# Loading two small tables from the same DMA queue as the data, ahead of it

## Chip, cores, metric

One core of a Trainium2 chip; the other cores are idle. The metric is the device time of one execution in microseconds (us), the median of several executions. A profile of one execution is read beside it; its span, counted from the first instruction, is some 2 us shorter than the time.

## The reference

The input `x` has shape (16, 512, 16, 64) in float32, 33.6 MB. `cos` and `sin` have shape (512, 32), 64 KB each. Only the first 32 values of each head are rotated; the other 32 are copied.

```python
x1, x2 = x[..., :32], x[..., 32:]
first  = x1[..., :16] * cos[..., :16] - x1[..., 16:] * sin[..., :16]
second = x1[..., :16] * sin[..., :16] + x1[..., 16:] * cos[..., :16]
return np.concatenate([first, second, x2], axis=-1)
```

All of `x` has to be read and all of the output written: 67.1 MB.

## The kernel before

`x` is cut into 8 tiles of 4 MB, 128 partitions by 32 KB. A tile is loaded through SP's DMA queue, rotated in place on VectorE in two halves (two products, a difference and a sum each), and stored through ACT's queue. Five buffers rotate, so the first five loads need not wait for a store. The tables are loaded once, through ACT's queue, and spread by VectorE into `table`.

```python
stage = const_pool.tile([PB, 2, K, HF], fp32)            # PB = 64 partitions
nc.scalar.dma_start(out=stage[:, 0]..., in_=cosf)        # ACT's queue
nc.scalar.dma_start(out=stage[:, 1]..., in_=sinf)
table = const_pool.tile([P, 2, K, 2, Q], fp32)
# ... four tensor_copy of stage into table ...
for t in range(T):                                       # 8 tiles
    x_t = x_pool.tile([P, K, H, D], fp32)                # bufs=5
    nc.sync.dma_start(out=x_t..., in_=xf[t])             # SP's queue
    for k0 in range(0, K, KC):
        # ... a = x1*c; b = x1*s; x1 = a-b | a+b, on VectorE ...
    nc.scalar.dma_start(out=of[t], in_=x_t...)           # ACT's queue
```

Of the kernel before, what the change touches and what calls it, by code (L numbers as in the profile page):

```python
# [1 line left out]

# [4 lines left out]


@with_exitstack
def kernel(  # L10
    ctx: ExitStack,
    tc: tile.TileContext,
    x: bass.AP,
    cos: bass.AP,
    sin: bass.AP,
    out: bass.AP,
):
    nc = tc.nc
    fp32 = mybir.dt.float32
    P = 128  # L20
    B, S, H, D = x.shape
    Q = D // 4
    HF = D // 2


    K = 8
    T = B * S // (P * K)
    PB = S // K
    REP = P // PB

    xf = x.rearrange("b s h d -> (b s h d)").rearrange("(t p f) -> t p f", t=T, p=P)
    of = out.rearrange("b s h d -> (b s h d)").rearrange("(t p f) -> t p f", t=T, p=P)
    cosf = cos.rearrange("(p k) j -> p (k j)", k=K)
    sinf = sin.rearrange("(p k) j -> p (k j)", k=K)

    const_pool = ctx.enter_context(tc.tile_pool(name="const", bufs=1))
    x_pool = ctx.enter_context(tc.tile_pool(name="xp", bufs=5))
    ab_pool = ctx.enter_context(tc.tile_pool(name="abp", bufs=1))

    stage = const_pool.tile([PB, 2, K, HF], fp32)  # L40
    nc.scalar.dma_start(out=stage[:, 0].rearrange("p k j -> p (k j)"), in_=cosf)  # L41
    nc.scalar.dma_start(out=stage[:, 1].rearrange("p k j -> p (k j)"), in_=sinf)


    table = const_pool.tile([P, 2, K, 2, Q], fp32)
    for r in range(REP):
        for t in range(2):
            nc.vector.tensor_copy(  # L48
                out=table[r * PB : (r + 1) * PB, t],
                in_=stage[:, t, :, 0:Q].unsqueeze(2).to_broadcast((PB, K, 2, Q)),  # L50
            )
    C = table[:, 0].rearrange("p k c j -> p k (c j)")
    Sn = table[:, 1].rearrange("p k c j -> p k (c j)")

    KC = 4
    for t in range(T):
        x_t = x_pool.tile([P, K, H, D], fp32)
        nc.sync.dma_start(out=x_t.rearrange("p k h d -> p (k h d)"), in_=xf[t])  # L58
        for k0 in range(0, K, KC):
            x1 = x_t[:, k0 : k0 + KC, :, 0:HF]  # L60
            c = C[:, k0 : k0 + KC].unsqueeze(2).to_broadcast((P, KC, H, HF))
            s = Sn[:, k0 : k0 + KC].unsqueeze(2).to_broadcast((P, KC, H, HF))
            a_t = ab_pool.tile([P, KC, H, HF], fp32)
            b_t = ab_pool.tile([P, KC, H, HF], fp32)
            nc.vector.tensor_mul(out=a_t[:], in0=x1, in1=c)  # L65
            nc.vector.tensor_mul(out=b_t[:], in0=x1, in1=s)  # L66
            nc.vector.tensor_sub(  # L67
                out=x1[:, :, :, 0:Q], in0=a_t[:, :, :, 0:Q], in1=b_t[:, :, :, Q:HF]
            )
            nc.vector.tensor_add(  # L70
                out=x1[:, :, :, Q:HF], in0=a_t[:, :, :, Q:HF], in1=b_t[:, :, :, 0:Q]
            )
        nc.scalar.dma_start(out=of[t], in_=x_t.rearrange("p k h d -> p (k h d)"))


# [1 line left out]
_INS = ['x', 'cos', 'sin']  # L77
_OUTS = [((16, 512, 16, 64), 'float32')]


# [23 lines left out]
```

## Time and profile before

| | before |
|---|---|
| time, median of 3 | 162.38 us (162.28 to 162.39) |
| VectorE busy | 110.8 us, 69% of the span |
| data moved, mean rate | 67.25 MB, 419 GB/s |
| first and last DMA packet (packet records) | 1.73 us, 159.2 us |
| one 32 KB packet on one of 16 DMA engines, median | 1.213 us, so 432 GB/s for all 16 |

From the page of the kernel before: the span; VectorE's busy time; then three rows with one entry for each of 40 slices of the span (VectorE's and the DMA engines' busy share in tenths, and the GB/s moved); then the chain of work that ended last, by engine and by line.

```profile
span 160.4 us, 155 instructions
...
DVE 110.8 (69%) x68; POOL 0.2 (0%) x4
...
DVE  0001599999999999999998799609995099940000
...
DMA  7999999999999999999999999999999999999993
GB/s 253 408 400 408 392 417 490 400 408 498 400 400 474 433 392 457 457 392 449 466 392 417 490 400 408 498 400 400 476 425 400 466 441 400 449 457 400 417 482 147
...
DMA 53%; DVE 30%; issue 4%; DVEq 1%; ACTq 0%; SPq 0%
DMA x_t<-in_x_dram 21%; DMA out_dram<-x_t 21%; DVE b_t L66 11%; DMA stage<-in_sin_dram 10%; DVE a_t L65 10%; DVE x_t L70 5%; DVE x_t L67 4%; DVEq L99 1%; ACTq L41 0%; DVE table L48 0%; SPq L58 0%; DVEq L65 0%
```

The DMA row is the one to read. It is at 9 in every slice but the first and the last: the 16 engines have no spare time. VectorE's row is empty for the first three slices and has gaps later. An idle VectorE costs something only if it leaves the DMA engines without work. The chain also names the load of sin (10%), which is what draws the eye to the tables. Single slices of the GB/s row swing by some 10 to 15% because the engines' 32 KB packets run nearly in step.

VectorE's waits in the kernel before: who waited for what, us in total, times, longest.

```profile
DVE a_t L65 <- DMA x_t<-in_x_dram: 13.2, 3, 5.9
DVE table L48 <- DMA stage<-in_cos_dram: 12.2, 1, 12.2
DVE table L48 <- DMA stage<-in_sin_dram: 4.9, 1, 4.9
```

The start of the timeline before: start in us, duration in us, engine, line, operation; in brackets the idle time before it and what ended it. A `q` marks an engine's sequencer issuing a DMA.

```profile
0.73 0.54 ACTq L41 DMA_DIRECT2D stage<-in_cos_dram  x1
0.73 11.78 SPq L58 DMA_DIRECT2D x_t<-in_x_dram  x5
1.30 0.61 ACTq L42 DMA_DIRECT2D stage<-in_sin_dram  x1
12.19 0.59 DVE L48 COPY table<-stage 64x256 f32<-64x256 f32 x2 [12.19 <-DMA stage<-in_cos_dram]
17.67 0.59 DVE L48 COPY table<-stage 64x256 f32<-64x256 f32 x2 [4.90 <-DMA stage<-in_sin_dram]
18.29 2.29 DVE L65 TENSOR_TENSOR a_t<-x_t,table 128x2048 f32<-128x2048 f32 x1
...
32.14 0.35 ACTq L73 DMA_DIRECT2D out_dram<-x_t  x1
```

SP and ACT start to issue at the same moment, 0.73 us. The tables land at 12.2 and 17.6 us, and the first product starts at 18.29 us. Tile 0 of `x` had landed at 13.62 us. The first store is issued at 32.14 us.

DMA issues before: KB each, and the median time from issue to landing in us.

```profile
x_t<-in_x_dram SPq DMA_DIRECT2D x8, 4096.0 KB, 33.9
out_dram<-x_t ACTq DMA_DIRECT2D x8, 4096.0 KB, 31.3
stage<-in_cos_dram ACTq DMA_DIRECT2D x1, 64.0 KB, 11.4
stage<-in_sin_dram ACTq DMA_DIRECT2D x1, 64.0 KB, 16.3
```

A 64 KB table needs 11 to 16 us. The packet records say why: its first packet runs at 5.95 us, behind three 32 KB packets of `x` on each engine (48 have started by then on the 16 engines), and after that each engine mostly runs one 1 KB table packet (46 ns) and then one of `x`.

### The profile page before, as it was taken

To read this page: it belongs to the slowest core of one execution; us is meant where nothing else is said; L and a number is where in the kernel's file an instruction comes from. 1 tells how busy PE (TensorE), PEld (TensorE's weight loads), DVE (VectorE), ACT (ScalarE), POOL (GpSimd) and SP (SyncE) were. 2 spreads that over 40 slices of the span, in tenths; PEclk is the share of its full clock that TensorE was granted. 3 is DMA by queue.
4 is the path that set the end of the run, shared out by engine and by line. 5 is a ranking of instruction groups with operands and counts; after the bars stand their busy time and mean duration, and the time that the engine had idled before them with its cause. 6 is when DMAs were issued, how large, how long until landed. Compare 5 with 4: busy or idle time off the path is not lost.

```text
span 160.4 us, 155 instructions
## 1 busy us (share of the span) xinstructions
DVE 110.8 (69%) x68; POOL 0.2 (0%) x4
## 2 busy tenths in 40 slices
DVE  0001599999999999999998799609995099940000
POOL 0000000000000000000000000000000000000000
DMA  7999999999999999999999999999999999999993
GB/s 253 408 400 408 392 417 490 400 408 498 400 400 474 433 392 457 457 392 449 466 392 417 490 400 408 498 400 400 476 425 400 466 441 400 449 457 400 417 482 147
DMA packets 2465, 67.25 MB, mean 419 GB/s; under 512 B 288, under 2 KB 416, under 8 KB 416
## 3 DMA queue, kind: packets, MB, share of 16 engines
q1 hardware_dynamic: 1152, 33.55, 49.3%
q10 hardware_dynamic: 1312, 33.69, 48.7%
q14 instruction: 1, 0.01, 0.0%
HBM read 33.69 MB, written 33.55 MB: 419 GB/s over the span
## 4 chain that ended last, share of the span: by engine, by line
DMA 53%; DVE 30%; issue 4%; DVEq 1%; ACTq 0%; SPq 0%
DMA x_t<-in_x_dram 21%; DMA out_dram<-x_t 21%; DVE b_t L66 11%; DMA stage<-in_sin_dram 10%; DVE a_t L65 10%; DVE x_t L70 5%; DVE x_t L67 4%; DVEq L99 1%; ACTq L41 0%; DVE table L48 0%; SPq L58 0%; DVEq L65 0%
## 5 line engine op out<-in xcount | busy, mean ns | idle before, releaser
L65 DVE TENSOR_TENSOR a_t<-x_t,table 128x2048 f32<-128x2048 f32 x16 | 36.7, 2292 | 13.6 <-DMA x_t<-in_x_dram 13.2
L66 DVE TENSOR_TENSOR b_t<-x_t,table 128x2048 f32<-128x2048 f32 x16 | 36.5, 2284 | 0.0
L67 DVE TENSOR_TENSOR x_t<-a_t,b_t 128x1024 f32<-128x1024 f32 x16 | 19.6, 1226 | 0.6
L70 DVE TENSOR_TENSOR x_t<-a_t,b_t 128x1024 f32<-128x1024 f32 x16 | 19.5, 1218 | 0.0
L48 DVE COPY table<-stage 64x256 f32<-64x256 f32 x4 | 1.1, 287 | 17.1 <-DMA stage<-in_cos_dram 12.2
L88 POOL MEMSET const-bfloat16-1.0<- 128x1 bf16 x1 | 0.1, 102 | 0.0
L88 POOL MEMSET const-uint8-127<- 128x1 uint8 x1 | 0.1, 102 | 0.0
L88 POOL MEMSET const-float32-0.0<- 128x1 f32 x1 | 0.1, 99 | 0.2 <-issue 0.2
L88 POOL MEMSET const-float32-1.0<- 128x1 f32 x1 | 0.1, 99 | 0.0
## 6 DMA issues: line engine op xcount, KB each, us to landing
x_t<-in_x_dram SPq DMA_DIRECT2D x8, 4096.0 KB, 33.9
out_dram<-x_t ACTq DMA_DIRECT2D x8, 4096.0 KB, 31.3
stage<-in_cos_dram ACTq DMA_DIRECT2D x1, 64.0 KB, 11.4
stage<-in_sin_dram ACTq DMA_DIRECT2D x1, 64.0 KB, 16.3
```

Of the source, the lines that this page charges most:

```text
L48: nc.vector.tensor_copy(out=table[r * PB : (r + 1) * PB, t], in_=stage[:, t, :, 0:Q].unsqueeze(2).to_broadcast((PB, K, 2, Q)),)
L65: nc.vector.tensor_mul(out=a_t[:], in0=x1, in1=c)
L66: nc.vector.tensor_mul(out=b_t[:], in0=x1, in1=s)
L67: nc.vector.tensor_sub(out=x1[:, :, :, 0:Q], in0=a_t[:, :, :, 0:Q], in1=b_t[:, :, :, Q:HF])
L70: nc.vector.tensor_add(out=x1[:, :, :, Q:HF], in0=a_t[:, :, :, Q:HF], in1=b_t[:, :, :, 0:Q])
L88: nc = _bacc.Bacc("TRN2", target_bir_lowering=False, num_devices=1)
L99: with _tile.TileContext(nc) as tc:
```

## The change

The intent is to have the tables before the first tile of `x`, so that VectorE, and with it the first store, starts earlier. Both table loads move from ACT's queue to SP's, ahead of the loads of `x`.

```diff
     stage = const_pool.tile([PB, 2, K, HF], fp32)
-    nc.scalar.dma_start(out=stage[:, 0].rearrange("p k j -> p (k j)"), in_=cosf)
-    nc.scalar.dma_start(out=stage[:, 1].rearrange("p k j -> p (k j)"), in_=sinf)
+    nc.sync.dma_start(out=stage[:, 0].rearrange("p k j -> p (k j)"), in_=cosf)
+    nc.sync.dma_start(out=stage[:, 1].rearrange("p k j -> p (k j)"), in_=sinf)
```

## The prediction

> **What bounds the kernel now.** The 16 DMA engines. The page's DMA row shows 9 tenths in all slices but the first and last, and 419 GB/s over the span of 160.4 us. In the trace's packet records the first packet starts at 1.73 us and the last ends at 159.2, with hardly a gap; summed packet time is 157.0 us per engine. A 32 KB packet takes 1.213 us on one engine, so 16 engines move 432 GB/s. That is near the 435 GB/s fabric ceiling in the Trainium skill, page "DMA: Bandwidth & Descriptors", section "Where 436 GB/s comes from"; this trace agrees. 2048 such packets over 16 engines are 155.3 us. VectorE is busy 110.8 us (69%): not the limit.
>
> The chain of waits does begin with the sin table (16.3 us, until 17.65), and the list of waits has VectorE waiting 12.2 us for cos and 4.9 us for sin, although x tile 0 landed at 13.62 us. That wait is the change's aim.
>
> **What the change does.** It adds and removes no work. The table issues move from ACT's queue to SP's, ahead of the x loads.
> - Before, SP's first x issue and ACT's cos issue both started at 0.73 us, and the first x packet ran 1.0 us later. Now x follows two table issues. An x issue took 0.33 us alone and 0.37 to 0.67 in company, so I estimate that x starts 0.7 to 0.9 us later.
> - The table packets (128 of 1 KB, 46 ns each: 0.37 us per engine) fill part of that gap; before, they ran between x packets. The net loss of about 0.4 us is on the critical path, since DMA is saturated from there to the end.
>
> Gain: tables land at about 4 us, so the first product starts when x tile 0 lands, about 14.3 us instead of 18.3, and the first store is issued at about 28.3 us instead of 32.1.
>
> **What that is worth.** Nearly nothing. Earlier stores take turns with loads on full engines: the same page, section "Issuing engines are not separate DMA queues", says that transfers of all queues interleave on the same engines. The trace agrees: 432 GB/s in loads alone, about 216 + 216 mixed, 433 in stores alone. The loads therefore end later by about the 3.8 us by which stores start earlier: the last load lands near 132 us instead of 128.2, the last store is issued near 146 instead of 142.1. Its predecessor lands near 150 us (149.95 before), so the store queue still doesn't run dry: its slack shrinks from 7.8 to about 4 us.
>
> **Predicted time:** 162.7 us, range 162.0 to 163.5. Chances: faster by over 2% 0.01, within 2% 0.97, slower by over 2% 0.02.
>
> **What the profile would show if right.** VectorE's wait for tables shrinks from 17.1 to about 4 us, followed by some 10 us for x tile 0 and longer waits for later x tiles (about 20 us; 13.2 before). GB/s stay near 432 between start and end. The last packet ends 0 to 1 us later than 159.2. VectorE's busy time stays. The first slice moves less than 253 GB/s.
>
> **What would make it wrong.** If mixed traffic were faster than either alone, more overlap would save time. If the last store found its queue dry, that would show at the end. If 1 KB packets start slowly, x would start over 1 us late. If interleaved table packets cost x more than 0.37 us before, the change could win a few tenths.

## The result

| | before | after |
|---|---|---|
| time, median of 6 | 162.38 us | 163.94 us (163.86 to 164.08) |
| ratio | | 1.0098, interval 1.0085 to 1.0111 |
| VectorE busy | 110.8 us | 110.8 us |
| first store issued | 32.14 us | 28.30 us |
| last load lands | 128.20 us | 133.82 us |
| last store issued / lands | 142.14 / 159.59 us | 147.76 / 161.22 us |

A ratio is the mean time of one kernel's fast runs over the mean of the other's in the same rounds, so it isn't quite the ratio of the medians. The change costs 1.56 us, 1%. It is within 2%, as foretold, but outside the range of 162.0 to 163.5 us.

The same rows of the page, after:

```profile
span 162.1 us, 154 instructions
...
DVE 110.8 (68%) x68; POOL 0.2 (0%) x4
...
DVE  2004999999999899932999159980799609994000
...
DMA  6889999979899999899899999999999998998993
GB/s 162 388 388 437 469 388 445 404 324 509 388 429 477 388 437 469 388 461 445 388 477 429 388 477 429 396 485 412 396 487 404 404 501 388 437 469 388 437 469 137
...
DMA 56%; DVE 31%; issue 3%; DVEq 1%; SPq 1%
DMA x_t<-in_x_dram 34%; DMA out_dram<-x_t 22%; DVE b_t L66 11%; DVE a_t L65 10%; DVE x_t L70 5%; DVE x_t L67 5%; DVEq L99 1%; SPq L42 0%; SPq L41 0%; DVEq L65 0%; SPq L58 0%
```

VectorE starts a slice earlier, as intended, and its busy time is the same. Two slices of the GB/s row stand out: the first (162 instead of 253), and the ninth, from 32.4 to 36.5 us (324, where no inner slice was below 392 before). The first is the start; the ninth is where the packets of the first store begin.

VectorE's waits after, and the start of the timeline:

```profile
DVE a_t L65 <- DMA x_t<-in_x_dram: 33.1, 6, 10.3
DVE table L48 <- DMA stage<-in_cos_dram: 2.8, 1, 2.8
```

```profile
0.73 0.54 SPq L41 DMA_DIRECT2D stage<-in_cos_dram  x1
1.33 0.57 SPq L42 DMA_DIRECT2D stage<-in_sin_dram  x1
1.95 2.63 SPq L58 DMA_DIRECT2D x_t<-in_x_dram  x5
2.84 1.28 DVE L48 COPY table<-stage 64x256 f32<-64x256 f32 x4 [2.84 <-DMA stage<-in_cos_dram]
14.46 2.29 DVE L65 TENSOR_TENSOR a_t<-x_t,table 128x2048 f32<-128x2048 f32 x1 [10.34 <-DMA x_t<-in_x_dram]
...
28.30 0.38 ACTq L73 DMA_DIRECT2D out_dram<-x_t  x1
```

The wait for the tables shrank from 17.1 us to 2.8 us, and the wait for `x` grew from 13.2 to 33.1 us: the wait was changed for another. The price is in the third line. SP spends 0.54 and 0.57 us on the two table issues, so the first load of `x` is issued at 1.95 us, 1.22 us later than before.

DMA issues after:

```profile
x_t<-in_x_dram SPq DMA_DIRECT2D x8, 4096.0 KB, 42.0
out_dram<-x_t ACTq DMA_DIRECT2D x8, 4096.0 KB, 31.5
stage<-in_cos_dram SPq DMA_DIRECT2D x1, 64.0 KB, 2.1
stage<-in_sin_dram SPq DMA_DIRECT2D x1, 64.0 KB, 2.2
```

The tables land in about 2 us. The median load of `x` takes 42.0 us instead of 33.9: the loads now share the engines with stores from earlier on.

### Where the time went: an account of lost time

All engines being busy from start to end, the useful question is when they moved less than 432 GB/s. From the packet records, take at any time T the bytes moved by then (a packet under way counted in part) and subtract bytes/432 GB/s from T. That is the time lost so far, as a mean over the 16 engines. It grows where the engines stand still or are slow, and stays level elsewhere.

```
time lost by T, us                  before   after   difference
T =   6 us  (start)                  2.61    3.83      1.22
T =  18 us  (tables in the stream)   3.25    3.81      0.56
T =  28 us                           3.26    3.78      0.52
T =  36 us  (first store)            3.27    4.80      1.53
T =  60 us                           3.21    4.74      1.53
T = 150 us                           3.07    4.58      1.51
```

Three steps make up the whole: +1.22 us at the start, -0.66 us between 6 and 18 us, where the tables no longer run between packets of `x`, and about +1.0 us at the first store. From 36 us to the end the kernels run alike. The sum of 1.5 us is the measured 1.56 us to within 0.1.

The last step was in nobody's sum. The packet records don't name the engine, but they can be strung together, since on one engine each packet starts when the one before ends. One such string around the first store (start in us; L a load and S a store; duration in ns):

```
before  32.51 L 1218   33.73 L 1213   34.94 L 1216   36.15 S 1213   37.36 L 1216
after   28.01 L 1213   29.22 L 1213   30.43 L 1596   32.02 L 2169   34.19 S 1213
```

In the kernel after, two load packets per engine around the first store packet are stretched, here the two ahead of it by 0.4 and 1.0 us; it is much the same in the other strings, save that in a few of them the second one comes just behind the first store packet. There are 34 load packets of over 1.26 us in this stretch of time, and what they take beyond 1.213 us adds up to 1.02 us per engine. In the kernel before, none is over 1.26 us. Once stores run, loads and stores take turns packet by packet in both kernels, each at 1.213 us (160 loads and 160 stores start between 36 and 60 us, in both). That turn-taking is what the Trainium skill, page "DMA: Bandwidth & Descriptors", section "Queues, rings and completion order", states of the engines' arbitration between queues, and these strings agree.

### The profile page after: what moved, and what is told of

Read it like the earlier page. It is cut to its first block, busy times and chain, and to the rows that moved or that the text cites. A ratio compares the mean times of both kernels' runs of the same rounds, so it can differ in the third digit from the quotient of the medians.

```text
span 162.1 us, 154 instructions
## 1 busy us (share of the span) xinstructions
DVE 110.8 (68%) x68; POOL 0.2 (0%) x4
## 4 chain that ended last, share of the span: by engine, by line
DMA 56%; DVE 31%; issue 3%; DVEq 1%; SPq 1%
DMA x_t<-in_x_dram 34%; DMA out_dram<-x_t 22%; DVE b_t L66 11%; DVE a_t L65 10%; DVE x_t L70 5%; DVE x_t L67 5%; DVEq L99 1%; SPq L42 0%; SPq L41 0%; DVEq L65 0%; SPq L58 0%
## 5 line engine op out<-in xcount | busy, mean ns | idle before, releaser
L65 DVE TENSOR_TENSOR a_t<-x_t,table 128x2048 f32<-128x2048 f32 x16 | 36.7, 2292 | 33.4 <-DMA x_t<-in_x_dram 33.1
L66 DVE TENSOR_TENSOR b_t<-x_t,table 128x2048 f32<-128x2048 f32 x16 | 36.5, 2283 | 0.0
```

What stands on the lines that cost most here:

```text
L65: nc.vector.tensor_mul(out=a_t[:], in0=x1, in1=c)
L66: nc.vector.tensor_mul(out=b_t[:], in0=x1, in1=s)
```

## The experiments

Two questions: does the late start cost what the account says, and what is the stretch at the first store? Each run is described with its edit against the kernel after, unless said. "Start", "stream" and "first store" are the time lost by 6 us, from there to just before the first store, and around it, from the account above.

### The change again

No edit.

> The changed kernel unaltered, for a second trace. Theory A (cold queue): the loss at the first store comes from the ACT queue being used for the first time in the program; it must recur: about 51 packets of x longer than 1.26 us, about 1.0 us lost per DMA engine within 30 to 36 us, total 163.9 us. Theory B (accident of one profile): the slow packets are gone or elsewhere, and the time is unchanged.

Measured 164.01 us, ratio 1.0096 (1.008 to 1.0111). Start 3.78, first store 1.25 us. The stretch is there again: 32 load packets over 1.26 us long between 29 and 35 us, against 34 in the first trace (the 51 of the expectation count those of the start, too). Theory B, an accident of one profile, falls.

### A small load on ACT's queue at the start

```diff
+    warm = const_pool.tile([16, K * HF], fp32)
+    nc.scalar.dma_start(out=warm[:], in_=cosf[0:16])
```

> The changed kernel plus one 16 KB load on ACT's queue at the start, into a tile that nobody reads. Theory A (first use of the ACT queue costs about 1.0 us of all 16 engines, and costs it when there is traffic to slow): the dip near 30 to 36 us disappears and the time falls by about 0.5 to 1.0 us, to 163.0 to 163.4. Theory C (stores that start as early as 28 us disturb the loads, whatever queue was used before): the dip stays and the time stays at 163.9.

Measured 163.98 us, ratio 1.0097; first store 1.15 us. Having used ACT's queue once, for one 1 KB packet per engine ahead of the stream, doesn't help. As I had put it, theory A (the queue's first use) falls.

### Tile 0 of x first, then the tables, on SP's queue

```diff
+    nc.sync.dma_start(out=x_first..., in_=xf[0])
     nc.sync.dma_start(out=stage[:, 0]..., in_=cosf)
     nc.sync.dma_start(out=stage[:, 1]..., in_=sinf)
```

> The tables stay on SP's queue, but are issued after x tile 0 instead of before. Takes the delayed start away and leaves the ACT queue unused until the first store. Theory A: the start costs what it did before the change (about 2.6 us lost in the first 6 us instead of 3.8), the dip at the first store of about 1.0 us stays; 163.0 to 163.3 us. Theory D (all of the loss is the delayed start, and the dip is paid for elsewhere): back to 162.4 us.

Two of four executions were fast, 162.30 and 162.42 us (ratio 0.9997), and two slow, 167.68 and 175.24. The fast ones have all of the change's loss back. The profile fell in a slow execution, so it serves only for the stretch up to the first store, ahead of what makes that execution slow: start 2.70 (as before the change), stream 0.43, first store 0.18 us. That small loss at the first store I had not expected: theory A had a full 1.0 us there, since ACT's queue was unused here too. So theory A falls once more: by this trace, it isn't the first use of the queue that costs the 1.0 us. The time is the one that theory D had; where the stretch went stays to be asked.

### The change with a later first store

```diff
+            for _ in range(2):                 # ahead of the first product
+                nc.vector.tensor_copy(out=spare[:], in_=x_t[:, 0:KC, :, HF:D])
```

> The changed kernel with two VectorE copies ahead of the first product, so that the first store is issued at about 32.5 us as before the change. Theory A: the dip of about 1.0 us stays and moves with the store, to 34 to 40 us; 163.9 us. Theory C (the early store is what disturbs): the dip disappears, about 162.9 us.

The copies were shorter than I had reckoned, so the store was issued at 30.80 us, not 32.5. Measured 164.6 us. First store 0.61 us, with the stretched packets moved along to 32 to 36 us. The loss follows the store but is smaller, which neither theory said; another 0.7 us was lost in small pieces from 60 to 120 us, for which I have no cause. With four copies:

> The changed kernel with four VectorE copies ahead of the first product instead of two; first store at about 33.2 us, later than the 32.1 us of the kernel before the change; fifth x load still early. Theory C: no dip at the first store, about 162.9 to 163.3 us. Theory E: a dip of about 1 us stays, 163.9 us or more.

Store issued at 32.63 us, later than before the change. Measured 163.71 us, ratio 1.0085; first store 0.86 us, on packets from 33 to 37 us. Theory C, that an early store is the trouble, falls. So far E, about the fifth load, stood.

### The fifth load of x later

Four loads are issued at first; a small VectorE copy writes into the fifth buffer, so that its load waits for it.

```diff
+    first = [x_pool.tile([P, K, H, D], fp32, name="x_t") for _ in range(5)]
+    for i in range(4): nc.sync.dma_start(out=first[i]..., in_=xf[i])
+    nc.vector.tensor_copy(out=first[4][0:1, 0, 0, 0:HF], in_=first[0][0:1, 0, 0, HF:D])
+    nc.sync.dma_start(out=first[4]..., in_=xf[4])
```

> The changed kernel, but its fifth x load is issued only after x tile 0 has landed (about 14.5 us instead of 4.1; before the change it was 12.2, in the run with x tile 0 first 13.7). Theory E (five queued x loads make the first store costly): the dip of 1.0 to 1.2 us per engine at the first store disappears, time 162.8 to 163.0 us. Theory C (the store is early): dip and 163.9 us stay.

The load went out at 40.1 us, because the scheduler put the copy later than I had meant. Only four loads had been issued when the first store came. Measured 164.02 us, ratio 1.0101; first store 1.03 us. Theory E falls.

### No tables at all

Against the kernel before; the result is wrong.

```diff
-    nc.scalar.dma_start(out=stage[:, 0]..., in_=cosf)
-    nc.scalar.dma_start(out=stage[:, 1]..., in_=sinf)
+    nc.vector.memset(stage[:], 0.5)
```

> Wrong result on purpose: the kernel before the change with no table loads at all (the tables are set to a constant), so nothing delays the first x load, nothing runs between its packets, the ACT queue is unused until the first store, that store goes out at about 27.5 us and the fifth x load is issued early. Theories C and E: the dip of about 1 us shows, and the time is 162.4 - 0.6 + 1.0, about 162.7 us. Theory F (the dip needs table packets ahead of x on the same queue): no dip, about 161.7 us.

Measured 162.33 us against 162.34 before, ratio 0.9996 (0.9979 to 1.0012). Start 2.65, stream 0, first store 1.10 us. This is the most telling run. Without any table packets the stretch is there, so the change didn't create it; theory F falls by the trace. (The time lies between the two forecasts, 161.7 and 162.7 us, and decides nothing.) And taking away 128 KB of loads and their 0.65 us in the stream gains nothing, because the first store then takes about as much. From its page, the DMA and GB/s rows:

```profile
DMA  7999999999999999999999999999999999999993
GB/s 237 416 391 489 424 392 481 302 400 473 432 400 449 449 400 449 457 400 440 465 400 440 465 400 416 489 400 408 489 402 416 465 424 408 449 449 408 440 449 147
```

The first slice is near that of the kernel before (237; 253 there), so the start isn't late. The eighth (302) is the first store.

### Both of the earlier helps together

Tile 0 first, as above, and the small load on ACT's queue.

> x tile 0 first, then the tables, on SP's queue, plus the small unused load on ACT's queue; first store at about 29 us, fifth x load at about 13.7 us. Theory E: no dip, 162.3 us. Theory C: dip of about 1 us, 163.3 us. It also tells whether x tile 0 first shows its slow executions (168 and 175 us in two of four) again.

Two fast executions at 162.38 and 162.44 us, two slow ones at 172.71 and 175.44. In the (slow) trace up to the first store: start 2.64, stream 0.60, first store 0.05 us.

By now a pattern showed: the stretch at the first store was absent or small wherever table packets had run in the middle of the running stream of loads, and there the stream had lost 0.4 to 0.65 us. That is theory G.

### One more table load between tile 0 and tile 1

```diff
         nc.sync.dma_start(out=x_t..., in_=xf[t])
+        if t == 0: nc.sync.dma_start(out=spare[:], in_=cosf)    # unused
```

> The changed kernel plus one more 64 KB load of cos (never used) on SP's queue between x tile 0 and x tile 1, four 1 KB packets per engine in the middle of the running x loads. Theory G (the first foreign packets that enter the running stream of x loads cost every engine one stretched packet, once in a program, wherever they come; tables before the stream don't count): 0.4 to 0.6 us lost per engine at 13 to 16 us, and at most 0.2 us at the first store instead of 1.0; time 163.6 to 164.0, so the time hardly tells, the trace does. If G is wrong: both losses, about 164.5 us.

Three fast executions, 163.96 to 164.42 us, ratio 1.011 (1.0087 to 1.0134), one slow at 174.39; the profile is a fast one. Stream 0.21, first store 0.52 us. Four small packets per engine halve the stretch; G had said at most 0.2 us. In kind right, in size half. ACT's queue carries nothing here before the first store, and this trace is a fast one, so small packets on SP's queue alone lessen the stretch.

### One small packet per engine in the stream

A load of 16 rows on ACT's queue that waits for tile 0.

```diff
+            nc.vector.tensor_copy(out=warm[:, 0:HF], in_=x_t[0:16, 0, 0, HF:D])
+            nc.scalar.dma_start(out=warm[:], in_=cosf[0:16])
```

> The changed kernel plus one 16 KB load (one 1 KB packet per engine) on ACT's queue, issued after x tile 0 has landed, so it enters the running stream at about 18 us. Theory G in its strong form (any foreign packet is enough): a small loss at 15 to 20 us, at most 0.2 us at the first store, time 163.0 to 163.7. Weak form (it takes several): the stretch of about 1.0 us at the first store stays, 163.95 us.

Measured 163.85 us, ratio 1.0089; stream 0, first store 1.18 us. One packet isn't enough: the strong form of G falls.

### The kernel before again

> The kernel before the change, unaltered, for a second trace. Expected: again 0.6 us lost per engine between 8 and 18 us while the table packets run between x packets, and under 0.05 us at the first store; 162.4 us.

One execution, 162.60 us. Start 2.69, stream 0.40, first store 0.00 us. The loss in the stream varies (0.65 in the first trace), the absence at the first store doesn't. This trace lost less on average than the first one, yet its last packet ended later (159.64 us against 159.19): the mean over engines isn't the slowest engine, and differences of 0.2 us or so can't be settled by the account.

### Tile 0 first, again

> x tile 0 first, then the tables, on SP's queue, again, because the profile of the first try fell in a slow execution. Expected of a fast one: 2.6 to 2.7 us lost per engine in the first 6 us, about 0.4 to 0.6 us at 12 to 16 us, at most 0.2 us at the first store; 162.3 to 162.5 us in the fast executions, and some slow ones of 165 to 175 us.

Fast executions at 162.30 and 162.35 us, slow ones at 172.56 and 175.15; the profile was slow again. Up to the first store: start 2.67, stream 0.36, first store 0.32 us, somewhat above what I expected.

### The late start alone

Tile 0 first, tables after it, but two unused table loads ahead of both.

```diff
+    nc.sync.dma_start(out=spare[:, 0], in_=cosf)     # unused
+    nc.sync.dma_start(out=spare[:, 1], in_=sinf)     # unused
     nc.sync.dma_start(out=x_first..., in_=xf[0])
     nc.sync.dma_start(out=stage[:, 0]..., in_=cosf)
     nc.sync.dma_start(out=stage[:, 1]..., in_=sinf)
```

> x tile 0 first and then the tables, all on SP's queue, but with two unused 64 KB loads ahead of x tile 0: the late start of the change alone, with the tables kept in the middle of the stream. Theory S+G (the 1.56 us are a late start of about 1.1 us and a first-store stretch that is 0.3 to 0.5 us dearer than the table packets in the stream were): 1.1 to 1.2 us lost more than before by 6 us, under 0.35 us at the first store, fast executions 163.4 to 163.7 us. If the late start cost only the 0.4 us of the prediction: 162.8 us.

Only one of four executions was fast, 164.07 us; the others took 169 to 176 us, and there is no ratio. I had forgotten that the unused loads themselves move 128 KB, 0.3 us at 432 GB/s. With it, 162.31 + 1.22 + 0.3 gives 163.83, near the one fast execution, and far from the 162.8 of a cheap start. In the (slow) trace up to the first store: start 3.83 (late as in the change), stream 0.66, first store 0.06 us. The start is settled mainly by the traces: 3.74 to 3.87 us lost in all ten in which every load of `x` is issued behind two small loads, 2.61 to 2.70 in the seven in which the first is not.

### Eight small packets back in the stream

```diff
+            for i in range(2):                 # t == 0, after tile 0 has landed
+                nc.vector.tensor_copy(out=spare[:, i, 0:HF], in_=x_t[0:PB, 0, 0, HF:D])
+                nc.scalar.dma_start(out=spare[:, i], in_=cosf)
```

> The changed kernel plus two unused 64 KB loads on ACT's queue after x tile 0 has landed: eight 1 KB packets per engine that run between x packets, as the tables did before the change, with the late start kept. Dose reading of G (1 small packet per engine left 1.15 us at the first store, 4 left 0.5, 8 left 0.0 to 0.3): 0.4 to 0.7 us lost while they run, under 0.2 us at the first store; 163.5 to 163.9 us. If not G: 1.0 us at the first store on top, about 164.4 us.

Measured 164.24 us, ratio 1.0108 (1.0091 to 1.0125); this run moves 128 KB more, too. All executions are fast. The account: 3.81 us at 19 us, 4.49 at 31 us, 4.51 at 36 us. So 0.68 us are lost while the small packets run between load packets and in the load packets under way when they end (they start at 18.7 us, and the last ends at 29.65 us), and 0.02 us after that, when the first store comes. The cut at 31 us is a choice: the store had been issued at 28.58 us, and counted from the end of the last small packet the loss is 0.12 us, against 1.0 us in the kernel after from 28 us on. A string from this run:

```
27.61 S   46   27.65 L 1329   28.98 S 54   29.03 L 1349
30.38 L 1236   31.61 L 1226   32.83 S 1213  34.04 L 1213
```

(The S of 46 and 54 ns here are small loads on ACT's queue.) The load packets ahead of the first 32 KB store packet are hardly stretched. This is the same kernel as the change, with the same late start and a store issued at 28.58 us (28.30 in the change); all that was added is small packets in the stream (and two small copies on VectorE), and in the trace the stretch is nearly gone. The time doesn't confirm it. 164.24 us lies between the two forecasts, neither of which counted 0.3 us for the added bytes, and the 0.3 us that the account finds saved against the kernel after should have paid for just these bytes, at 163.9 us; the intervals of the two ratios overlap. Its DMA and GB/s rows:

```profile
DMA  5899999999999899999999999998999999999993
GB/s 161 379 395 436 472 399 399 391 436 460 395 436 468 387 468 436 395 484 411 428 460 403 436 460 395 436 468 387 460 438 395 476 419 436 452 403 444 452 395 137
```

The slot that read 324 in the kernel after, the ninth, reads 436 here; the loss is spread over the slices before it.

### Tile 1 from ACT's queue

```diff
-        nc.sync.dma_start(out=x_t..., in_=xf[t])
+        (nc.scalar if t == 1 else nc.sync).dma_start(out=x_t..., in_=xf[t])
```

> The changed kernel with x tile 1 loaded from ACT's queue at the start, so that 32 KB load packets of both queues take turns from about 4 us and the ACT queue has carried large packets before the first store, which comes at about 37 us. If the stretch belongs to a second queue's first large packets: none at the first store, at most 0.2 us. If it belongs to the first stores as such, entering a stream of loads alone: about 1.0 us there all the same. Time 163.0 in the first case, 163.9 in the second.

Measured 162.61 us, ratio 1.0018 (1.0001 to 1.0034). Start 2.63: ACT issues its load of `x` at 0.73 us while SP is busy with the tables, so the late start is gone. The tables then run in the stream (6 to 13 us), where 0.36 us are lost, and the first store loses 0.44 us. Neither of my two answers, none or 1.0 us, came out. 32 KB packets had come through ACT's queue long before, so a second queue's first large packets don't explain it all; but the tables in the stream disturb the test, and it stays inconclusive on queue against direction.

### The runs side by side

```
us lost per engine        small packets in    start   stream   first
                          the stream/engine                    store
before                           8             2.61    0.65     0.00
before, again                    8             2.69    0.40     0.00
after                            0             3.83    0        1.01
after, again                     0             3.78    0        1.25
small load at the start          0             3.74    0        1.15
fifth load late                  0             3.81    0        1.03
store later (2 copies)           0             3.87    0        0.61
store later (4 copies)           0             3.74    0        0.86
no tables                        0             2.65    0        1.10
one small packet                 1             3.80    0        1.18
one table between tiles          4             3.80    0.21     0.52
eight on ACT's queue             8             3.84    0.68     0.02
tile 1 on ACT's queue            8             2.63    0.36     0.44
traces of slow executions, up to the first store only:
tile 0 first                     8             2.70    0.43     0.18
tile 0 first, again              8             2.67    0.36     0.32
tile 0 first + small load        8             2.64    0.60     0.05
late start alone                 8             3.83    0.66     0.06
```

The traces above the line carry the argument: with none or one small packet in the stream the first store costs 0.6 to 1.25 us, with eight 0 to 0.44. The later rows agree. The loss isn't abolished but paid elsewhere in part: stream and first store together come to 0.40 to 0.80 us with four or eight small packets, and to 0.61 to 1.25 us with none or one.

## Why the prediction was wrong

- **The bound: right.** The DMA engines were the limit. VectorE started 3.8 us earlier, and the first store was issued at 28.30 us (predicted 28.3), and neither gained anything. That 28.3 came out so exactly is partly luck: `x` started later than foretold, but tables between its packets had cost tile 0 more than foretold, too, so it landed at 14.36 us (foretold 14.3). That a 17 us wait at the head of the chain is worth nothing here is shown best by the run without tables: 162.33 us.
- **Late start: right in kind, too small.** Foretold: `x` 0.7 to 0.9 us later. Measured: the first packet of `x` at 3.17 us instead of 1.73, 1.44 us later. Of this, 1.22 us are the two issues (0.54 and 0.57 us, and short pauses), and 0.21 us the issue of `x` itself (0.58 us instead of 0.37). I had costed a table's issue like one of a large load, some 0.35 to 0.45 us, although the trace before showed the same two table issues at 0.54 and 0.61 us on ACT; I put that down to company on the other queue, and they took nearly as long without any. The prediction did name a start over 1 us late among what would make it wrong, but for another reason, 1 KB packets that start slowly.
- **What the tables cost in the stream: too small.** Foretold: 0.37 us, the time of their own packets. They had cost 0.65 us (0.40 in the second trace) on top of 0.30 us for their bytes at the full rate, since the load packets between them were stretched, too. The two errors have opposite signs, so that by luck start and tables together came to 0.52 us net, near the 0.4 foretold.
- **The step that failed** is "GB/s stay near 432 between start and end", with its reason that "Earlier stores take turns with loads on full engines". They do, but not at once: about 1.0 us per engine is lost as the first store comes in, and the kernel before didn't pay it. 1.22 - 0.66 + 1.0 makes the 1.5 to 1.6 us measured; the last packet ended at 160.81 us, 1.6 us later than before (foretold 0 to 1).
- **Later steps: right in the main.** The last load landed at 133.82 us (foretold near 132). The store queue didn't run dry: the last store was issued at 147.76 us (foretold 146), and its predecessor landed at 151.58, a slack of 3.8 us (foretold about 4). The wait for later tiles was 33.1 us with tile 0's 10.3, so 22.8 (foretold 20).

What is shown of the stretch: it comes at the first store, not at a fixed time (it moved with the store); a first store at any time from 27 to 33 us has it; it isn't tied to the tables' being ahead of `x`, to the fifth load, or to one earlier use of ACT's queue; and eight small packets per engine in the stream take nearly all of it away in the trace, with the late start and early store left in place. So, as far as the traces show, the slow landing of the tables in the kernel before wasn't pure loss: their 0.65 us stood in for the 1.0 us at the first store.

What stays open is the mechanism. One observation bears on it: in the kernel after, 306 of 307 load packets between 6 and 29.4 us took 1213 ns; in the kernel before, between the last table packet and the first store packet, they took 1213 to 1227 ns, and no large stretch follows. That could be something that the undisturbed stream has ahead and gives up once, gradually or at a stroke. This is a guess; no run shows what it is. Nor is it known why the versions with small loads right behind tile 0 on one queue run slow (167 to 176 us) in half of their executions (10 of 20 in five runs); in such traces the first and the last engine's completion of one store lie up to 15 us apart (at most 2.7 us in the other traces). No version tried beats the kernel before.

## What to carry to other kernels

When the DMA engines are full from the first microsecond, an idle compute engine at the start is not a loss to recover, and whatever is issued on the same queue ahead of the first large load delays everything: here 0.54 to 0.57 us for each small load, on the only path that counted. The page "DMA: Bandwidth & Descriptors" of the Trainium skill, section "Issuing engines are not separate DMA queues", says that issuing from several engines "will only save the time on the sequencer it takes to initiate the DMA". Test a supposed waste by taking it out altogether (wrong result, one run) before moving it: the run without tables would have told that there was nothing to win.

## What the Trainium skill lacked or had wrong

- "DMA: Bandwidth & Descriptors", section "Latency and other measured facts", gives about 600 ns to the first byte for this kind of DMA. It doesn't say from where that counts. Here the first packet record came 1.0 us after the start of the first issue for a load of `x` (0.73 to 1.73 us) and 1.3 us for a table (0.73 to 2.05 us). From the end of the issue it is 0.63 us for `x` and 0.78 us for the table, so the page fits if the issue itself is left out.
- The same page calls the issue's time small, and no page gives it by queue or shape: the runs show 0.33 us for a large load issued alone, 0.36 to 0.9 us in a row of issues, and 0.47 to 0.61 us for a 64 KB table load in 64 rows.
- No page has the stretch of load packets as the first store enters a stream of loads alone: 0.6 to 1.25 us per engine, once per execution, and 0 to 0.12 us where eight 1 KB packets per engine had been spread between the load packets (0.44 us in the run where tile 1 came from ACT's queue, 0.05 to 0.32 us in traces of slow executions).
- The same page, section "Where 436 GB/s comes from", says that the HBM side, about 358 GB/s, binds transfers between HBM and SBUF, next to its fabric figure of 435. For a core that works alone that sentence is too low, and the page's own measurement beside it, 425 GB/s with one core, says so, too. Loads alone, stores alone and the mixture all ran at 432 GB/s here, with one core at work.
- No page tells of the slow executions of the versions with small loads right behind tile 0 on the same queue: 167 to 176 us in 10 of 20 executions, instead of 162.3 to 164.4.
